# Two-layer hybrid trunk on one core: the duration estimate of a TensorE product has 32 columns added, and four planned moments are moved

## The chip, the core and the metric

The kernel runs on one core of a Trainium2 chip. The time is the device time of one execution in microseconds (us); "before" is the median of three runs. The core has TensorE (PE) for matrix products and transposes, VectorE (DVE), ScalarE (ACT) and GpSimd (POOL) for everything elementwise, and SyncE (SP), which here issues most of the DMA transfers. Each engine works through its own instruction list strictly in order; engines wait for each other by semaphores.

## The reference, cut to what matters

The input is one sequence of 512 tokens with 1024 features, float32, and two layers of parameters. Each layer computes

```
h = rmsnorm(x, norm_g);  p = h @ w_in                    # 1024 -> 3488 columns, split into 15 pieces
A: q = rmsnorm(cq) @ w_uq;  k, v = rmsnorm(ckv) @ w_ukv   # 4 heads, rope, causal softmax attention
B: o_b = c_b * short_conv(c_c * c_h, conv_w)              # width 3
C: o_c = u * (tril(sg_w) @ layernorm(v) + sg_b)           # in chunks of 128 tokens
D: q, k, v = mq, mk, mv                                   # 4 heads, rope, block-sparse attention (MoBA)
y = concat(o_a*silu(g_a), o_b*silu(g_b), o_c*silu(g_c), o_d*silu(g_d))
x = x + y @ w_out
```

Query blocks have 128 rows. With blocks of 256 keys and 512 tokens, group D's choice of blocks comes out as causal attention too.

## The kernel before, in words

**Products.** Every factor is split into a high part and a low part in the fp32r type, and each product is three PE instructions: high by high, high by low, low by high (`mm3`, L282). PE thus has 2,423 products and transposes in its list, most of them over 512 columns (tokens), the low-rank products of group A over 416, spatial mixing and some others over 256, transposes over 128.

**Weights.** They come in units of about 512 KB. SP issues the load of a unit (`load_units`, L405; the DMA itself is at L295) into one of a few raw buffers, two for most units. ACT, or DVE, makes the high part (`whi_*`), DVE the low part (`wlo_*`), into one of six pairs of split buffers (`split_units`, L442). A raw buffer is free for the next load when its split is done. An instruction that waits for a load holds up everything behind it on its engine.

**Seven-product stages.** Three groups of large products, the output projection of both layers (products `oz`, `ox`, `oy`, `ot`; weights `b`, `t`) and the token products of layer 1 (weights `p`), use a scheme with seven half-size products instead of eight. It needs sums of weight blocks, which are made in DRAM by `t_sums` (L356): SP copies a block (L367) and POOL issues accumulating DMAs onto the copy (L372). This chain starts at the moment TS0 (L2051). The products of layer 0's output projection start at place 1055 in PE's list.

**The order of the work.** The program writes out all instruction lists at build time with a planner, the class `Order` (L74). Everything is a coroutine ("chain"). The planner has one clock, `now`, which is PE's: each PE instruction adds its estimated duration. `cost(n)` gives it for a product over n columns; transposes have 109 ns written beside them. ACT, DVE, POOL and DMA have clocks with estimates of their own (`act`, `dve`, `pool`, L166 on); these are not touched. A chain that has a PE instruction to issue does this:

```
def pe(self, cost, f, *a, **k):
    if self.t != self.pe_t:
        while self.t + PEMARGIN > self.o.now:
            yield self.t + PEMARGIN
...
    self.o.now += cost
```

`self.t` is the moment at which its operands are ready by plan, so the instruction is placed at the first moment at least 80 ns (PEMARGIN) later. Until then other chains place theirs: among those that are due, `run` (L108) takes the one with the lowest priority number. The main stream has 10: the projections in the fixed orders SEQ and SEQ1 (L48, L380) and the output products. The attention heads of A (scores `sa`, softmax `pa`, its transposes `pTa` with the copies `pha` and `pla`, output `oa`) and D (the same with `d`) and other small chains have 0, so they go first as soon as they are due, and the main stream fills the gaps. How many filler products stand between two steps of an attention head thus follows from the vector engines' estimates divided by the products' estimates. ACT's and DVE's lists follow from the same clock: an instruction is emitted when the chain comes within 300 ns (SLACK) of it.

Some chains have a moment in `now` at which they may start: the mixing of group C in layer 0 (MIXT, L1904), a row of parameters (ROWT, L781 and L2049), columns of parameters (COLT, L623 and L2041) and the weight sums (TS0, L2051). Places in a list below count PE instructions from the start of the kernel.

**Names used further on.** `raw_cc`, `whi_cc`: the weights of the piece c_c, loaded and split; likewise `ch`, `gc`, `gd`, `gb`, `su`, `kv`. `zz` is the product c_c * c_h of group B on DVE, which reads the PSUM bank of `cc`. `hT` is the transposed normalised input of a layer, `a` a copy of it, and `hTh`, `hTl` its two parts. `rs_mq`, `rs_mk` are the norms of D's queries and keys, with a power on POOL. `yad`, `yD`, `ys` and `suml` are outputs of the heads and their sums ahead of the output products.

Of the kernel before, what the change touches and what calls it, by code (L numbers as in the profile page):

```python
# [32 lines left out]
WSLACK = 0.0  # L33
AHEAD, URGENT, VSLACK = 4, 2, 300.0
NWARM, FILL, FILLEND = 6, 0.9, 15000.0
MIXT, MIXLAG, ROWT, COLT = 42000.0, 2000.0, 36000.0, 17500.0
KSPLIT, HMEAN = 6, 0.0
PAIRS = {}
LOPRIO = -5
# [8 lines left out]
SEQ1 = ['p11', 'ga0', 'p21', 'p3', 'ga1', 'p4', 'p2', 'ch0', 'p1', 'p22', 'cc0', 'gd0', 'gd1', 'su0', 'gc0', 'cb0', 'gb0', 'ch1', 'cc1', 'cb1', 'gb1', 'su1', 'gc1']  # L48
K0, K1, KK = (2, 3, 0, 1), (4, 5, 6, 7), (0, 2, 3, 1)
ZPROD = ("b11", "t3", "b21", "t4", "t2", "t1", "b22")  # L50
TS0 = 62000.0
TAIL = ((0, 256), (256, 512))

C_CQ, C_KV, C_GA, C_CH, C_CB, C_CC, C_GB = 0, 256, 416, 672, 928, 1184, 1440
# [111 lines left out]
class Chain:  # L166
# [6 lines left out]
    def _emit(self, e, cost, f, a, k):  # L173
        while max(self.t, self.o.clk[e] if self.lazy else 0.0) > self.o.now + self.slack:
            yield max(self.t, self.o.clk[e] if self.lazy else 0.0) - self.slack
        self.o.clk[e] = max(self.o.clk[e], self.t, self.o.now) + cost
        self.t = self.o.clk[e] + LAT
        f(*a, **k)  # L178
# [19 lines left out]
# [4 lines that stand above are left out]
        if self.o.now < self.o.fill_until:  # L202
            for _ in range(int((self.o.now - self.o.pe_end) * FILL / (430.0 if self.o.now < 9000.0 else 220.0))):
                self.o.fill()
        self.o.now += cost
        self.o.pe_end = self.o.now
        self.t = self.pe_t = self.o.now + PELAT
        f(*a, **k)  # L208
# [5 lines left out]


def cost(n):
    return max(n / 2.4, 107.0) + 2.0


@with_exitstack  # L220
def hybrid_trunk(ctx: ExitStack, tc: tile.TileContext, x, positions, norm_g, w_c, w_f, w_t, w_o, mla_q_norm_g,
# [60 lines left out]
    def mm3(ch, n, dst, sh, sl, mh, ml, first, last, go_on=False, low=None):  # L282

        c = cost(n)
        k = dict(skip_group_check=True) if go_on else {}
        yield from ch.pe(c, PE.matmul, dst, sh, mh, start=first, stop=False, **k)
        yield from ch.pe(c, PE.matmul, dst, sh, ml, start=False, stop=False, **k)
        if low is not None:
            yield from ch.wait(low)
        yield from ch.pe(c, PE.matmul, dst, sl, mh, start=False, stop=last, **k)  # L290
# [65 lines left out]
    def t_sums(*streams):  # L356

        gap = 4000.0 if len(streams) == 1 else 3000.0
        for i in range(3):
            steps = []  # L360
            for l, src, t, b in streams:
                for n, x, y in (((f"{t}1", f"{b}11", f"{b}12"), (f"{t}3", f"{b}12", f"{b}22")),
                                ((f"{t}2", f"{t}1", f"{b}22"),), ((f"{t}4", f"{t}2", f"{b}21"),))[i]:
                    steps += [(l, src, n, x, y, j) for j in range(2)]
            for l, src, n, x, _, j in steps:
                o.clk["D"] = max(o.clk["D"], o.now) + 1500.0
                nc.sync.dma_start(src(l, n, j), src(l, x, j))  # L367
                yield o.now + gap
            yield o.now + gap
            for l, src, n, _, y, j in steps:  # L370
                o.clk["G"] = max(o.clk["G"], o.now) + 1000.0
                nc.gpsimd.dma_start(src(l, n, j), src(l, y, j), accum_op=ALU.add, max_dma_last_dim=1024)  # L372
                o.set(tsum_ev[l, n, j], o.now + 10000.0)
                yield o.now + gap
            yield o.now + (8000.0 if len(streams) == 1 else 0.0)
# [1633 lines left out]
    def start():  # L2009
        o.clk["D"] = 1000.0  # L2010
        cw = Chain(o)
        for kp in range(KT // 2):
            xk[kp] = yield from v4S.get(cw, f"x{kp}_0", [P, NT, 2 * P], F32)
        load_xk(0, 1)
        wp = yield from sS.get(cw, "warm")
        ones = one_box[0][:, 0:P].bitcast(F32)
        V.memset(ones, 1.0)
        A.activation(xsum[:, 0, 0:1], ones[:, 0:1], AF.Square, scale=D ** -0.5)
        o.fill = lambda: PE.matmul(wp[:, 0:P], ones, ones, start=True, stop=True)
        for _ in range(NWARM):  # L2020
            o.fill()
        PE.transpose(wp[:, 256:256 + NT + KT], junk[0:NT + KT, P:2 * P], ident[0:NT + KT, 0:NT + KT])
        V.tensor_copy(pg, wp[:, 256:256 + NT + KT])
        o.pe_end, o.fill_until = 3700.0, FILLEND
        o.clk["V"] = 3700.0

        def fill_end():
            o.fill_until = 0.0
            sS.put(Chain(o))
            return  # L2030
            yield
        o.spawn(fill_end(), FILLEND, -9)
        LOAD_HOOKS["c0_0"] = (lambda: load_xk(2, 4),)
        LOAD_HOOKS["c1_0"] = (lambda: load_xk(4, 6),)
        LOAD_HOOKS["c2_0"] = (lambda: load_xk(6, 8),)
        prow.append((yield from t2S.get(cw, "prow")))
        G.memset(prow[0][0:14, 0:P], 1.0)
        LOAD_HOOKS["sq0_0"] = (load_rows,)
        LOAD_HOOKS["sq1_0"] = (lambda: load_params(L0, 0),)
        LOAD_HOOKS["sq3_0"] = (lambda: load_params(L0, 1),)  # L2040
        o.spawn(param_cols(), COLT, 2)  # L2041
        for u in order[:10]:
            u.wanted = True
        o.spawn(load_units(), None, 4)
        o.spawn(split_units(0, 4), None, LOPRIO)
        o.spawn(split_units(4, len(order)), None, 5)
        o.spawn(rope_tables(), 3700.0, 4)
        o.spawn(x_stats(), None, 5)
        o.spawn(x_row(), ROWT, 5)  # L2049
        o.spawn(main(), None, 10)  # L2050
    o.spawn(t_sums((0, z_src, "t", "b"), *((l, p_src, "p", "p") for l in STOK)), TS0, 4)  # L2051
    o.spawn(start())
# [51 lines left out]
```

## Time and profile before

| | |
|---|---|
| median of 3 runs | 489.70 us (489.56 to 489.83) |
| the profiled execution's own time | 489.73 us |
| its span, first to last instruction | 488.0 us |
| TensorE's granted clock | 0.999 |
| DMA traffic | 92.89 MB, mean 190 GB/s |

A row of the waits view has the engine and group that waited, the group that released it, and then the total, the number and the longest of the waits in us. A row of a timeline has the start and the duration in us, then the engine, line and operation, output <- inputs, shapes, and in brackets the idle time before it with what ended it; consecutive equal instructions are one row with a count. Instructions of one engine overlap by their pipelines, so the cost of one in a steady stream is the distance from start to start. In the view by groups, "x | a, b" is the count, the busy time in us and the mean in ns. In the view by windows, a row has the window and its length, the busy times (with counts) of PE, its weight loads, DVE, ACT and POOL, and last the granted clock, the DMA engines' busy share and GB/s. In the view of DMA issues, the last two numbers are the size and the median time from issue to landing in us. In the chain of work that ended last, a row is the start, the length, and what ran.

### The profile page before, as it was taken

The numbers are of one execution on the slowest core, as the hardware profiler recorded it, in microseconds if no ns is written. First come the engines' busy times: TensorE is split into PE (matmuls) and PEld (weight loads), VectorE is DVE, ScalarE is ACT, GpSimd is POOL, SyncE is SP. The second block draws the span as 40 slices with busy tenths as digits, with TensorE's granted clock in tenths as the row PEclk, the third lists the DMA queues.
The fourth block names the chain that finished last, engine by engine and source line by source line (L and its number), as shares of the span: only waits on it lengthen the run. The fifth ranks groups of instructions, "written<-read, shape, count | busy, mean of one in ns | idle before, by whom it ended". The sixth has DMA issues, their size and how long they took to land.

```text
span 488.0 us, 7509 instructions
## 1 busy us (share of the span) xinstructions
PE 481.6 (99%) x2432; PEld 408.9 (84%) x2432; DVE 400.9 (82%) x893; ACT 329.9 (68%) x898; POOL 104.4 (21%) x172
## 2 busy tenths in 40 slices
PE   9999999999999999999999999999999999999997
PEld 7988888888887888888889988888888888888786
DVE  3698487668987899789998688979788998997993
ACT  5896837677546766457667788769675687666650
POOL 7855330710051210000031013620402200000000
PEclk9999999999999999999999999999999999999999
DMA  8742335897499888596574186786832744427762
GB/s 263 249 135 78 124 128 218 225 197 162 151 330 240 208 217 218 188 343 224 199 239 145 65 290 250 165 246 177 209 131 85 153 136 146 173 66 258 253 242 89
DMA packets 41904, 92.89 MB, mean 190 GB/s; under 512 B 7158, under 2 KB 23048, under 8 KB 41480
## 3 DMA queue, kind: packets, MB, share of 16 engines
q1 hardware_dynamic: 29168, 79.82, 47.3%
q0 software_dynamic: 12672, 12.58, 16.7%
q8 instruction: 19, 0.31, 0.2%
q14 instruction: 21, 0.17, 0.1%
q10 hardware_dynamic: 24, 0.01, 0.0%
HBM read 84.53 MB, written 33.03 MB: 241 GB/s over the span
## 4 chain that ended last, share of the span: by engine, by line
PE 91%; DVE 3%; ACT 2%; DMA 2%; SPq 1%; issue 1%; ACTq 0%
PE oy L208 6%; PE cq L208 6%; PE kv L208 6%; PE gb L208 5%; PE su L208 5%; PE cc L208 5%; PE sq L208 5%; PE gc L208 5%; PE ch L208 5%; PE ga L208 4%; PE oz L208 4%; PE cb L208 4%; PE py L208 3%; PE ox L208 3%; PE sa L208 3%; PE gd L208 3%
## 5 line engine op out<-in xcount | busy, mean ns | idle before, releaser
L178 ACT ACTIVATE pa<-pa,mna 128x128 f32<-128x128 f32 (+3 forms) x53 | 27.8, 554 | 5.6 <-DVE mna L178 5.5
L178 ACT ACTIVATE pd<-pd,mnd 128x384 f32<-128x384 f32 (+3 forms) x49 | 25.8, 548 | 3.2 <-DVE mnd L178 2.9
L178 ACT ACTIVATE pha<-pTa 128x512 fp32r<-128x512 f32 (+3 forms) x32 | 13.9, 434 | 20.6 <-PE pTa L208 20.4
L178 ACT ACTIVATE phd<-pTd 128x512 fp32r<-128x512 f32 (+3 forms) x32 | 13.8, 434 | 16.1 <-PE pTd L208 15.9
L178 DVE CUSTOM_DVE_ANT_0 pa<-sa,maskb,rs_q 128x512 f32<-128x512 f32 (+3 forms) x32 | 16.6, 544 | 6.2 <-PE sa L208 3.2
L178 DVE TENSOR_TENSOR wlo_p<-raw_p,whi_p 128x512 fp32r<-128x512 f32 x28 | 19.1, 698 | 2.7 <-ACT whi_p L178 2.6
L178 ACT ACTIVATE whi_t<-raw_t 128x512 fp32r<-128x512 f32 x31 | 18.2, 619 | 4.5 <-DMA raw_t<-t 4.5
L208 PE MATMUL cq<-whi_c,hTh 128*128 128x416 f32 x64 | 20.8, 370 | 0.0
L178 DVE TENSOR_TENSOR wlo_t<-raw_t,whi_t 128x512 fp32r<-128x512 f32 x32 | 20.7, 679 | 0.0
L208 PE MATMUL cq<-wlo_c,hTh 128*128 128x416 f32 x64 | 20.0, 359 | 0.0
L178 DVE TENSOR_TENSOR pla<-pTa,pha 128x512 fp32r<-128x512 f32 (+3 forms) x32 | 15.4, 485 | 5.6 <-ACT pha L178 5.6
L208 PE MATMUL cq<-whi_c,hTl 128*128 128x416 f32 x64 | 19.8, 355 | 0.0
L178 POOL TENSOR_TENSOR rs_mk<-rs_mk,nhalf 128x16 f32<-128x16 f32 x2 | 6.5, 3243 | 56.3 <-DVE rs_mk L178 56.3
L178 DVE CUSTOM_DVE_ANT_0 pd<-sd,maskb,rs_mq 128x512 f32<-128x512 f32 (+3 forms) x32 | 17.0, 545 | 1.6 <-PE pTd L208 1.0
L178 DVE TENSOR_TENSOR pld<-pTd,phd 128x512 fp32r<-128x512 f32 (+3 forms) x32 | 15.1, 485 | 3.1 <-ACT phd L178 3.0
L178 POOL TENSOR_SCALAR xss<-xss 128x1 f32<-128x1 f32 x4 | 2.7, 668 | 69.6 <-ACT jk L178 65.3
L372 POOL DMA_DIRECT2D t<-in_w_o_dram x16 | 17.0, 1341 | 2.4 <-DMA t<-t 2.3
L178 DVE TENSOR_TENSOR wlo_b<-raw_b,whi_b 128x512 fp32r<-128x512 f32 x24 | 16.0, 682 | 0.1
L178 ACT ACTIVATE whi_b<-raw_b 128x512 fp32r<-128x512 f32 x23 | 13.9, 622 | 3.1 <-DMA raw_b<-in_w_o_dram 3.0
L178 ACT ACTIVATE whi_p<-raw_p 128x512 fp32r<-128x512 f32 x22 | 13.2, 625 | 3.9 <-DMA raw_p<-in_w_t_dram 3.9
L208 PE MATMUL pTd<-ident,pd 128*128 128x128 f32 x80 | 14.1, 272 | 0.6 <-ACT pd L178 0.6
L208 PE MATMUL pTa<-ident,pa 128*128 128x128 f32 x80 | 14.0, 273 | 0.0
(473 smaller groups left out, 1846.8 us busy)
## 6 DMA issues: line engine op xcount, KB each, us to landing
t<-in_w_o_dram POOLq DMA_DIRECT2D x16, 512.0 KB, 8.3
raw_t<-t SPq DMA_DIRECT2D x16, 512.0 KB, 4.0
raw_b<-in_w_o_dram SPq DMA_DIRECT2D x12, 512.0 KB, 4.0
t<-in_w_o_dram SPq DMA_DIRECT2D x8, 512.0 KB, 4.9
p<-in_w_t_dram POOLq DMA_DIRECT2D x8, 512.0 KB, 14.0
t<-t SPq DMA_DIRECT2D x8, 512.0 KB, 4.7
raw_p<-p SPq DMA_DIRECT2D x8, 512.0 KB, 3.2
ys<-ysc SPq DMA_DIRECT2D x14, 256.0 KB, 5.0
```

What stands on the lines that cost most here:

```text
L178: f(*a, **k)
L208: f(*a, **k)
L372: nc.gpsimd.dma_start(src(l, n, j), src(l, y, j), accum_op=ALU.add, max_dma_last_dim=1024)
```

## The change

`cost(n)` becomes (n+32)/2.4 ns, at least 108, instead of n/2.4, at least 107, plus 2. For 512 columns that is 226.7 instead of 215.3, for 416 186.7 instead of 175.3, for 384 173.3 instead of 162, for 256 120 instead of 109, for 128 108 instead of 109. The four moments given in the planner's clock are raised as well (MIXT and TS0 by 4.8%, ROWT by 4.7%, COLT by 2.9%). Transposes keep 109, and the estimates of the other engines, the margins and the end of the warm-up filling (FILLEND, 15000) stay as they are.

```diff
-MIXT, MIXLAG, ROWT, COLT = 42000.0, 2000.0, 36000.0, 17500.0
+MIXT, MIXLAG, ROWT, COLT = 44000.0, 2000.0, 37700.0, 18000.0
...
-TS0 = 62000.0
+TS0 = 65000.0
...
 def cost(n):
-    return max(n / 2.4, 107.0) + 2.0
+    return max((n + 32) / 2.4, 108.0)
```

The products, the main stream's order, the transfers and what is computed stay the same. What changes is how the side chains' instructions are interleaved with the main stream on each engine, and for a few splits and squares which of ACT and DVE does them (ACT's list has 3 instructions less, DVE's one more).

## The prediction

> **What bounds the kernel now.** I read the page's first part, then the cores, the waits of TensorE (PE), and the chain that ended last.
>
> ```profile
> core 0: 488.0 us, clock 0.999
> PE 481.6 (99%) x2432; PEld 408.9 (84%) x2432; DVE 400.9 (82%) x893; ACT 329.9 (68%) x898; POOL 104.4 (21%) x172
> ```
>
> ```profile
> PE warm L2019 <- DVE ones L2017: 1.1, 1, 1.1
> PE pTd L208 <- ACT pd L178: 0.6, 1, 0.6
> PE sq L208 <- ACT krt L178: 0.6, 1, 0.6
> PE gd L208 <- DVE zz L178: 0.3, 1, 0.3
> PE oz L208 <- DVE wlo_b L178: 0.3, 1, 0.3
> ```
>
> PE is busy for 481.6 of 488.0 us at full clock. Its work is fixed, and only order can change the time: these five waits are nearly all that order costs now. The chain gives the true price of a product (start, duration, group):
>
> ```profile
> 16.28 2.26 PE cq L208 x12
> ```
>
> ```profile
> 61.03 10.88 PE ga L208 x48
> ```
>
> ```profile
> 481.72 2.88 PE ot L208 x24
> ```
>
> 10.88/48 is 226.7 ns for 512 columns, 2.26/12 is 188 for 416, 2.88/24 is 120 for 256. The old estimate says 215.3, 175.3 and 109; the new one 226.7, 186.7 and 120. So the planner's clock ran about 5% slow and is now right. Transposes keep 109, near enough: two sets of four follow each other after 0.44 us, 0.11 each.
>
> ```profile
> 73.83 0.60 PE L208 MATMUL t0a<-ident,Q 128*96 128x128 f32 x4
> 74.27 0.60 PE L208 MATMUL t1a<-ident,K 128*96 128x128 f32 x4
> ```
>
> **The change, part by part.** Nothing is added or removed on PE: both builds issue the same 2,423 products and transposes, and the same DMAs. I compared the two built instruction lists engine by engine, and turned distances in PE's list into time with the prices above.
>
> The moved moments (MIXT, ROWT, COLT, TS0) grow by 3 to 5%, as the clock does; the transposes, products and copies that they release stand at about the same products as before. I cost them at 0: PE's steady stream covers them.
>
> The longer estimate makes a product of a side chain come due after fewer products of the main stream, since the vector work between is priced as before. The attention chains get thinner in filler and finish earlier. In layer 0 the last MLA attention product goes from place 681 to 636, MoBA's from 1023 to 954 (the next stage starts at 1055). In layer 1 MLA's goes from 2003 to 1944; MoBA starts later there and ends at 2245 instead of 2260. The start of the kernel, with the first and third of the five waits, is unchanged. The other three are at places that the new order alters.
>
> *Place 1, 157 us.*
>
> ```profile
> 157.17 0.27 PE L208 MATMUL pTd<-ident,pd 128*128 128x128 f32 x1
> 158.04 0.55 PE L208 MATMUL pTd<-ident,pd 128*128 128x128 f32 x3 [0.60 <-ACT pd L178]
> ```
>
> ```profile
> 155.02 0.63 ACT L178 ACTIVATE whi_cc<-raw_cc 128x512 fp32r<-128x512 f32 x1 [2.69 <-DMA raw_cc<-in_w_f_dram]
> ```
>
> ```profile
> 148.47 6.53 DMA raw_cc<-in_w_f_dram
> ```
>
> ```profile
> raw_cc<-in_w_f_dram SPq DMA_DIRECT2D x4, 512.0 KB, 3.4
> ```
>
> The second transpose should start 0.11 after the first, at 157.28; it starts at 158.04, so 0.76 is lost. ACT, in order, stood 2.69 us before a weight split whose load took 6.53 us instead of the usual 3.4, with the attention copies queued behind it. In the built lists 17 products (3.6 us) of PE stand between that load's issue and its split before, and 33 (6.0 us) after. The 2.4 us more bring ACT's wait from 2.69 down to about 0.3; here the queue took up 2.69-0.76 = 1.93 before PE stood, so I take -0.76. If the load is longer by those 1.6 us, up to 0.76 stays.
>
> *Place 2, 343 us.* A product into gd takes the bank that the convolution's zz reads out of cc:
>
> ```profile
> 342.92 0.60 PE L208 MATMUL pTa<-ident,pa 128*128 128x128 f32 x4
> 343.86 0.50 PE L208 MATMUL gd<-hTh,whi_gd 128*128 128x512 f32 x1 [0.35 <-DVE zz L178]
> 344.20 0.40 PE L208 MATMUL gd<-hTl,whi_gd 128*128 128x512 f32 x1
> ```
>
> ```profile
> 343.12 0.69 DVE L178 SCALAR_TENSOR_TENSOR zz<-cc,chs 128x512 f32<-128x512 f32 x1 [0.25 <-PE cc L208]
> ```
>
> The four transposes end their turn at 342.92+0.44 = 343.36; gd starts at 343.86 (0.50 late) and its first product takes 0.34 instead of 0.227: 0.61. After, 21 products (3.26 us) stand between the last cc and this gd instead of the four transposes, and zz's 0.69 us lies beside them: -0.61.
>
> *Place 3, 458 us.*
>
> ```profile
> 457.62 0.61 PE L208 MATMUL oz<-whi_b,yD 128*128 128x512 f32 x2
> 458.50 0.50 PE L208 MATMUL oz<-wlo_b,yD 128*128 128x512 f32 x1 [0.26 <-DVE wlo_b L178]
> 458.83 0.40 PE L208 MATMUL oz<-whi_b,yD 128*128 128x512 f32 x1
> ```
>
> ```profile
> 450.48 0.68 DVE L178 TENSOR_TENSOR yad<-od,obd 64x512 f32<-64x512 f32 x1 [0.21 <-ACT obd L178]
> ```
>
> ```profile
> 456.82 0.41 DVE L178 TENSOR_TENSOR ys<-ys 128x256 f32<-128x256 f32 x1
> 457.16 0.68 DVE L178 TENSOR_TENSOR suml<-ys,sumh 128x512 fp32r<-128x512 f32 x1
> 457.76 0.68 DVE L178 TENSOR_TENSOR wlo_b<-raw_b,whi_b 128x512 fp32r<-128x512 f32 x1
> ```
>
> Due at 457.62+2x0.227 = 458.07, the product starts at 458.50 and takes 0.33: 0.43+0.10 = 0.53. VectorE (DVE) works back to back from the last attention output, 0.60 us from start to start per 512 columns and 0.34 per 256. After, 18 such instructions (13x0.60+5x0.34 = 9.5 us) stand between the last attention product and this one, but 52 products (11.8 us) instead of 37 (8.4 us): covered, -0.53.
>
> Removed: 0.76+0.61+0.53 = **1.90**.
>
> *New waits.* The cover of three other places gets short. (a) Layer 1's first hT transposes, near 245 us: ScalarE (ACT) has six instructions in the same 3.26 us of products instead of four. Prices, start to start:
>
> ```profile
> 250.83 0.55 ACT L178 ACTIVATE whi_c<-raw_c 128x416 fp32r<-128x416 f32 x1
> 251.26 0.60 ACT L178 ACTIVATE a<-hT 128x512 f32<-128x512 f32 x1
> 251.74 0.61 ACT L178 ACTIVATE oy<-xr 128x512 f32<-128x512 f32 x1
> ...
> 252.35 0.60 ACT L178 ACTIVATE hTh<-hT 128x512 fp32r<-128x512 f32 x1
> ```
>
> whi_c 0.43, a 0.48, oy 0.61, and hTh as a (both 0.60 long): two hTh (the first begun before the stretch, some 0.2 of it inside), two whi_c, oy and a's full 0.60 come to about 3.2 to 3.3 us. (b) The second attention product of layer 1's MLA head 2 and (c) of layer 0's MoBA head 1 stand closer behind their splits. Each is between 0 and 0.3 us, the length of the two DVE waits above; it cannot be a gain, since none of the three waits now. I take the middle: 3x0.15 = **+0.45**. A late load is a rarer kind of wait; it is between 0 and place 1's 0.76 at each place, taken as 0 here, and its other end is the second rival.
>
> DVE's load is the other worry, as denser attention asks more of it per product:
>
> ```profile
> 65.00:195.00 130.00, 129.40 (x677) 109.53 (x676) 106.76 (x249) 84.58 (x211) 25.93 (x25) 1.00 0.84 215
> ```
>
> 106.76 of 130 us is 82%; 5% more is 86%, so queues lengthen in places only.
>
> Sum against the profiled run, whose 489.73 are the span's 488.0 and 1.73 around it that the change doesn't touch: 489.73-1.90+0.45 = 488.28, and since that run lies 0.03 above the median of 489.70, **488.3** us.
>
> **A rule of the Trainium skill that speaks against the change.** "TensorE: Matmul & The Clock Gate", section "Back-to-back issue gap", gives an isolated warm gap of N/2.4+2.5 ns (216 for N=512), and less, some 131, for a sustained stream. By that the old estimate is right or too long, and the change makes every loop 5% too dense. The trace's 226.7 ns disagrees, and the measurement decides.
>
> **The rivals.**
>
> *As many waits as before.* The three gaps are accidents of one order, and another order has its own. Slack shrinks by 5% in all attention loops, so beyond (a) to (c) some three more waits of 0.3 to 0.6 us arise: 488.3+1.4 = 489.7. For it: every loop is touched. Against: PE stops only three times for order now, and I found three short covers, not six.
>
> *Slower, by late loads.* The POOL queue runs an attention step and behind it the accumulating copies for the later seven-product stages:
>
> ```profile
> 88.64 2.91 POOL L178 TENSOR_TENSOR rs_mq<-rs_mq,nhalf 128x16 f32<-128x16 f32 x1 [22.57 <-DVE rs_mq L178]
> 91.50 4.41 POOL L372 DMA_DIRECT2D t<-in_w_o_dram  x4
> 94.30 5.75 POOL L372 DMA_DIRECT2D p<-in_w_t_dram  x4
> ```
>
> ```profile
> t<-in_w_o_dram POOLq DMA_DIRECT2D x16, 512.0 KB, 8.3
> ```
>
> ```profile
> p<-in_w_t_dram POOLq DMA_DIRECT2D x8, 512.0 KB, 14.0
> ```
>
> In the new order that step comes some 8 us of products earlier, so these copies run beside the loads of gc0 and ch0. gc0's split on ACT stands only 3.6 us of products behind its load: if loads take 6.5 us again, ACT blocks as at place 1, for up to 0.76 of PE each time. It decides from three such blocks on (2.3 us against the 1.45 gained; 490.6), and with four it gives 491.3. I put it at 491.0. For it: the DMA engines are 84% busy in this stretch (next to last column). Against: in the old order this one load alone stopped PE.
>
> *The change does not do what it says:* by the page's rule the clock would now run 5% fast, loops would be too dense, and a wait of 0.3 us, the length of place 3's, would appear in about half of the 16 heads: 488.3+2.4 = 490.7. Against it stand the three products' prices above.
>
> **How the numbers follow.** A measurement of this kernel tells about 0.2% (0.98 us) from no change: faster means under 488.72, slower over 490.68. Forecast 488.3: 0.48. As many waits: 0.31. Late loads: 0.20; a too dense clock: 0.01. So faster 0.48, same 0.31, slower 0.21. All three gaps gone with no new wait is 487.8, and one more small gap might go: low end 487.4. The high end takes in three to four late loads: 491.2. The forecast's own range is 487.8 to 488.7.
>
> **What would show it.** In the new profile's PE waits, the rows pTd on pd, gd on zz and oz on wlo_b are gone; warm and sq stay. If (a) to (c) are right, hT waits on an ACT copy near 245 us and oa or od on pla or pld, 0.1 to 0.3 us each. Layer 0's last od should end some 15 us sooner. The first rival shows as many short PE waits on DVE or ACT, the second as ACT whi waits on raw loads between 70 and 100 us with PE waits behind them. I would be wrong if PE's idle time grows, or if one wait, at a bank or a queue that I did not count, exceeds 1 us.

## The result: slower, and the profile after

The changed kernel takes 491.30 us (median of 14 runs, 490.34 to 494.34) against 489.71 of before (488.88 to 492.06): ratio 1.0038, 95% interval 1.0020 to 1.0055. The prediction said 488.3. The profiled execution took 490.93, with a span of 489.2 us. The runs of the changed kernel spread more than those of before, and the two longest (494.34 and 493.95) have a mean granted clock of 0.995 and 0.996; the last section comes back to that. One run of e7 below, 683.43 us at a granted clock of 0.656, is left out of its ratio.

The waits of TensorE in the changed kernel (engine, group, what released it; total, number, longest):

```profile
PE warm L2019 <- DVE ones L2017: 1.1, 1, 1.1
PE pTd L208 <- DVE pd L178: 1.1, 2, 0.6
PE sq L208 <- ACT krt L178: 0.7, 1, 0.7
PE cq L208 <- ACT hTh L178: 0.3, 1, 0.3
PE oy L208 <- DVE xr L178: 0.2, 1, 0.2
PE xT L208 <- DMA x<-in_x_dram: 0.2, 1, 0.2
```

The three waits that were forecast to go (pTd on ACT, gd, oz) are gone. Four others stand in their place. Where the time came from is best seen by three stretches, between fixed places in the trace's list of PE records (counted from 0, with the warm-up products, so these places are nine higher than the prediction's). Place 228 lies near 46 us, where the start of the kernel ends; 1220, near 247 us, is the first hT transpose of layer 1; 2431 is the last. Ahead of each of them both kernels have done the same products and transposes, in another order:

| start of | before | changed | difference of the stretch |
|---|---|---|---|
| place 228 | 46.33 | 46.53 | +0.20 |
| place 1220 | 246.34 | 247.50 | +0.96 |
| place 2431 | 484.31 | 485.50 | +0.03 |

**Layer 0.** Two transposes of one attention step come late, and what made them late is a load, just as at 157 us before. PE's timeline, then ACT's, then the chain of work:

```profile
146.59 0.39 PE L208 MATMUL gd<-hTh,wlo_gd 128*128 128x512 f32 x1
147.51 0.30 PE L208 MATMUL pTd<-ident,pd 128*128 128x128 f32 x1 [0.54 <-DVE pd L178]
148.36 0.60 PE L208 MATMUL pTd<-ident,pd 128*128 128x128 f32 x3 [0.55 <-DVE pd L178]
```

```profile
144.72 0.63 ACT L178 ACTIVATE whi_gb<-raw_gb 128x512 fp32r<-128x512 f32 x1 [2.73 <-DMA raw_gb<-in_w_f_dram]
```

```profile
136.19 8.50 DMA raw_gb<-in_w_f_dram
144.72 0.63 ACT whi_gb L178
145.35 1.49 ACT pd L178 x6
146.86 0.19 DVE mnd L178
147.08 0.29 DVE pd L178
147.36 0.66 DVE chs L178
148.02 0.29 DVE pd L178
148.36 0.60 PE pTd L208 x3
```

The first pTd is due at 146.59+0.227 = 146.82 and starts 0.69 late; the next is due 0.11 later and starts 0.74 late: 1.43 us. A load of gb that took 8.50 us held ACT for 2.73 us; the softmax steps of pd stood behind it on ACT, and the transposes wait for DVE's steps behind those. The load of cc, which cost 0.76 us at 157 us before and was to be relieved, indeed costs nothing any more. These two make +0.67; the other 0.3 of the stretch lies in steps of about 0.1 us and less.

**Layer 1.** gd and oz (1.14 us) are gone. In their place stand two hT transposes near 256 us (0.25 together), two score products and one product of oy:

```profile
394.33 0.39 PE L208 MATMUL gb<-hTh,wlo_gb 128*128 128x512 f32 x1
394.75 0.50 PE L208 MATMUL sd<-mk0d,mq0d 128*128 128x512 f32 x1
```

```profile
393.36 0.63 ACT L178 ACTIVATE whi_cb<-raw_cb 128x512 fp32r<-128x512 f32 x1
394.01 0.68 ACT L178 ACTIVATE mk0d<-tmkd,pcol 64x512 fp32r<-64x512 f32 x1
```

```profile
473.86 0.39 PE L208 MATMUL oy<-whi_t,suml 128*128 128x512 f32 x1
474.46 0.47 PE L208 MATMUL oy<-whi_t,sumh 128*128 128x512 f32 x1 [0.22 <-DVE xr L178]
```

The score product sd stands 0.19 late and its first product takes 0.11 more, since mk0d ran on ACT behind a weight split (the same again at 400 us: 0.29); oy starts 0.38 late. That is about 1.2 us for 1.14.

### The profile page after: what moved, and what is told of

Its sections match the earlier page's. It is cut to its first block, busy times and chain, and to the rows that moved or that the text cites. A ratio compares the mean times of both kernels' runs of the same rounds, so it can differ in the third digit from the quotient of the medians.

```text
span 489.2 us, 7512 instructions
## 1 busy us (share of the span) xinstructions
PE 482.0 (99%) x2432; PEld 407.5 (83%) x2432; DVE 401.8 (82%) x894; ACT 330.1 (67%) x891; POOL 106.0 (22%) x172
## 4 chain that ended last, share of the span: by engine, by line
PE 86%; DVE 7%; DMA 3%; ACT 2%; issue 1%; SPq 0%
PE cq L208 6%; PE kv L208 6%; PE oy L208 5%; PE sq L208 5%; PE su L208 5%; PE gb L208 5%; PE cb L208 5%; PE ga L208 4%; PE gc L208 4%; PE gd L208 4%; PE ch L208 3%; PE cc L208 3%; PE py L208 3%; PE sa L208 3%; PE oz L208 2%; PE pz L208 2%
## 5 line engine op out<-in xcount | busy, mean ns | idle before, releaser
L178 ACT ACTIVATE pd<-pd,mnd 128x512 f32<-128x512 f32 (+3 forms) x51 | 27.1, 556 | 2.7 <-DVE mnd L178 2.2
L178 ACT ACTIVATE pa<-pa,mna 128x128 f32<-128x128 f32 (+3 forms) x45 | 23.9, 553 | 3.8 <-DVE mna L178 3.5
L178 ACT ACTIVATE whi_p<-raw_p 128x512 fp32r<-128x512 f32 x25 | 14.9, 623 | 2.4 <-DMA raw_p<-in_w_t_dram 2.4
L208 PEld LDWEIGHTS pTd<-ident,pd 128*128 128x128 f32 x80 | 10.3, 140 | 4.8 <-issue 0.9
```

## The experiments

Time stretches in the table are worked out as above, each from one trace of its kernel; "0-228" is the start of place 228. The same work stands ahead of place 1220 in all twenty traces. Ahead of place 228, e2, e13 and e17 have one or two other products of 512 columns, and e14 another order. The expectations count the second stretch to place 1300, so it is given too, but not all kernels have done the same there: the changed kernel and e1, e3, e6, e8, e10 to e15, e17 and e18 have four transposes ahead of place 1300 where the others have four products of 416 columns. That makes their figure 0.4 us too small against the others'.

| kernel | 0-228 | 228-1220 | 1220-2431 | 228-1300 | span | median, ratio to before (95%) |
|---|---|---|---|---|---|---|
| before | 46.33 | 200.01 | 237.97 | 213.74 | 488.0 | 489.71 |
| changed | 46.53 | 200.97 | 237.99 | 214.82 | 489.2 | 491.30, 1.0038 (1.0020-1.0055) |
| e1 | 47.04 | 199.84 | 238.03 | 213.69 | 488.6 | 490.54, 1.0019 (1.0006-1.0031) |
| e2 | 45.81 | 200.58 | 238.05 | 214.30 | 488.2 | 489.75, 1.0004 (0.9993-1.0015) |
| e3 | 47.23 | 199.38 | 238.01 | 213.24 | 488.3 | 489.74, 0.9998 (0.9987-1.0010) |
| e4 | 46.17 | 199.23 | 238.03 | 212.95 | 487.1 | 489.29, 0.9993 (0.9983-1.0003) |
| e5 | 47.03 | 201.56 | 238.24 | 215.31 | 490.5 | 492.45, 1.0059 (1.0044-1.0073) |
| e6 | 46.05 | 205.15 | 239.49 | 218.97 | 494.4 | 495.97, 1.0136 (1.0107-1.0165) |
| e7 | 46.26 | 200.25 | 238.14 | 213.96 | 488.4 | 489.68, 0.9995 (0.9984-1.0006) |
| e8 | 45.67 | 206.20 | 238.01 | 220.06 | 493.6 | 494.05, 1.0089 (1.0067-1.0110) |
| e9 | 46.14 | 200.12 | 238.65 | 213.85 | 488.6 | 491.61, 1.0034 (1.0019-1.0049) |
| e10 | 47.49 | 200.47 | 237.97 | 214.32 | 489.6 | 491.03, 1.0029 (1.0017-1.0040) |
| e11 | 45.88 | 206.11 | 237.99 | 219.97 | 493.7 | 494.57, 1.0099 (1.0081-1.0117) |
| e12 | 46.53 | 199.00 | 237.99 | 212.85 | 487.2 | 488.83, 0.9984 (0.9975-0.9993) |
| e13 | 45.57 | 199.79 | 238.04 | 213.61 | 487.1 | 488.82 (one run) |
| e14 | 46.12 | 201.28 | 238.04 | 215.13 | 489.2 | 490.87 (one run) |
| e15 | 46.55 | 204.07 | 238.01 | 217.92 | 492.3 | 494.01, 1.0071 (1.0052-1.0089) |
| e16 | 46.22 | 200.10 | 237.99 | 213.82 | 488.0 | 490.38, 1.0006 (0.9995-1.0016) |
| e17 | 45.90 | 199.90 | 237.97 | 213.73 | 487.5 | 489.24, 0.9989 (0.9980-0.9998) |
| e18 (changed again) | 46.99 | 203.24 | 238.01 | 217.10 | 492.0 | 491.98, 1.0045 (1.0028-1.0062) |

The theories: **A**, a weight load beside the accumulating DMAs of the weight sums is late, holds ACT or DVE, and so PE; **B**, thinner attention loops by themselves; **C**, the moved moments. From e5 on, **S** stands for a loss in the start by the new order of ACT and DVE there.

### e1, e2: the estimate alone, the moments alone

e1 is the changed kernel with `MIXT, MIXLAG, ROWT, COLT = 42000.0, 2000.0, 36000.0, 17500.0` and `TS0 = 62000.0`; e2 is the kernel before with the four new values.

> The new estimate with the four old moments. Theory A (a late load): what costs time in the changed kernel is a weight load that runs beside the accumulating DMAs of the second weight sum; here those sums start at 62 instead of 65 us of the planner's clock, some three products of the main stream earlier against the loads, so the 1.44 us lost at 147 us (load of gb 8.5 us long, ScalarE held 2.7 us by it, two transposes of pd late) should change its place or size: 489.5 to 491. Theory B (thin loops: the longer estimate leaves 5% less filler in every attention loop, moments don't matter): the same time as the changed kernel, 491.3, with the pTd wait of 1.4 us in place. Theory C (the moved moments cost it): 489.7.

> The old estimate with the four new moments. Theory A: the sums start later against the old order, so the 0.76 us lost at 157 us moves to another load: between 489.0 and 490.5, with the gd (0.6) and oz (0.5) gaps of before unchanged. Theory B: as before, 489.7. Theory C: 491.3.

The lists of PE, ACT and DVE of e1 are those of the changed kernel, instruction by instruction (buffer numbers apart); only SP's and GpSimd's transfers come in another order. With that alone, ACT's wait for gb falls from 2.7 to 1.6 us and the loss at 147 us from 1.43 to 0.29:

```profile
ACT whi_gb L178 <- DMA raw_gb<-in_w_f_dram: 1.6, 1, 1.6
```

So that loss does not follow from the order of the engines alone (against B); the transfers that run beside the load decide it. What the estimate alone costs in e1's trace lies in the start (0.71 us); its layer 0 is as fast as that of before (199.84 against 200.01). The moments alone cost nothing (against C): e2 is where before is, with the pTd gap moved from 157 to 189 us (0.85). The ratios of e1 and the changed kernel have overlapping intervals, and one trace each says little about a load whose length changes from run to run (e18 below): the weight of the argument is on e3 and e12.

### e3, e4: the second sums' additions left out

```diff
-                nc.gpsimd.dma_start(src(l, n, j), src(l, y, j), accum_op=ALU.add, max_dma_last_dim=1024)
+                if i != 1:
+                    nc.gpsimd.dma_start(src(l, n, j), src(l, y, j), accum_op=ALU.add, max_dma_last_dim=1024)
```

> The changed kernel with the four accumulating DMAs of the second sums (t2, p2) left out; the copies stay, so the sums lack a term. Theory A: the load of gb falls from 8.5 us to 3.5 to 4.5, ScalarE's wait of 2.7 us and the two pTd waits go: 1.44 us less than the changed kernel, a span of about 487.8 instead of 489.2. Theory B: the pTd waits stay, 489.2.

> The kernel before with the same four accumulating DMAs left out. Theory A: the load of cc falls from 6.5 us to about 3.5, and the 0.76 us at 157 us go: a span of 487.2 instead of 488.0. Theory B: the pTd wait stays, 488.0.

The edit leaves out six of the 24 accumulating DMAs, four between 132 and 148 us and two in layer 1. As theory A said: in e3 the pTd waits and ACT's wait for gb are gone and places 228 to 1220 take 1.59 us less than in the changed kernel; in e4 the gap at 157 us is gone and they take 0.78 less than before, though by the medians e4 gains only 0.44 us, with an interval that takes in no gain. e3's median is 489.74 where the changed kernel has 491.30, though its start was 0.7 us slower in its trace. And without these additions the new order takes nearly as long in layer 0 as the old one (199.38 and 199.23): for theory B's thinner loops that leaves 0.15 us. The DMA rows of the kernel before for the 16 us around its late load (queue: packets, MB, share of the 16 engines) show how heavy these transfers are:

```profile
q0 software_dynamic: 2025, 2.02, 78.9%
q1 hardware_dynamic: 422, 1.81, 30.8%
```

The software queue carries the accumulating transfers (in e12, which has none, it moves nothing), the hardware queue the loads. Packet by packet the former are small (2.02 MB in 2,025), and the time of their packets adds up to 79% of all DMA engines' time, for about the bytes that the hardware queue moves with 31%.

### e5 to e8: the new estimate in parts of the kernel

```diff
-        self.o.now += cost
+        self.o.now += cost - (32 / 2.4 - 2.0) * (cost > 109.5 and not LO <= self.o.npe < HI); self.o.npe += 1
```

LO and HI are 0 and 205 in e5, 205 and 1290 in e6, 1290 and the end in e7, 205 and the end in e8; `npe` counts the planner's PE instructions.

> The new estimate for the first 205 PE instructions (some 41 us), the old one behind; moments 44000, 37700, 18000 and 64000 (shifted by what the clock gains up to there). Theory S (the new lists of ScalarE and VectorE cost 0.2 to 1.0 us in the start, since the second half of a weight unit's split now stands ahead of hTh and waits for the load): PE's place 228 comes at 46.4 to 47.2 us as in the three traces of the new lists, not at 45.8 to 46.3 as in the three of the old ones. The rest is an order of its own: 489.5 to 491. Rival (the start differs by chance between executions): place 228 at 45.8 to 46.3.

> The new estimate from PE instruction 205 to 1290 (the rest of layer 0), the old one before and behind; old moments but TS0 at 63000. Theory S: place 228 at 45.8 to 46.3 us. Theory A (late loads beside the second sums): a pTd wait of 0.3 to 1.4 us near 147 us, behind a load of gb or cc of over 6 us. Layer 1 as before: gd 0.6 and oz 0.5. In all 489.5 to 490.8. Theory B (thin loops) gives PE waits on DVE or ACT steps of attention in layer 0 that no load explains.

> The new estimate from PE instruction 1290 on; old moments. All lists are those of before up to there, so the start and the 0.76 us at 157 us are those of before. Theory B' (in layer 1 the change trades the gd and oz gaps, 1.14 us, for waits of hT, sd and oy, 1.23 us in the changed kernel's trace): 489.7, same as before. The prediction's count (three short covers of 0.15) would give 489.0.

> The new estimate from PE instruction 205 on; moments 42000, 36000, 17500 and 63000. Theory S: place 228 at 45.8 to 46.3 us and 0.7 us less than the new estimate everywhere with the same luck of the loads: 489.9 to 490.6. Rival (chance): 490.5 to 491.3.

*Start.* e5 reached place 228 at 47.03, e6 to e8 at 45.67 to 46.26, as theory S said. Six traces have the changed kernel's PE list up to there and ten the list of before. The new lists give 46.53 to 47.49 (mean 47.05), the old ones 45.67 to 46.55 (mean 46.18): **0.87 us**, of which the first profile happened to show only 0.20. The two PE lists are the same up to place 172, and behind it they take the same time up to 228 (12.49 us before and changed), so the loss lies ahead of that, where ACT's list differs from 10 us on.

e5's whole time, 492.45, is a miss all the same: behind the start its order loses 1.33 us at 159 us, behind a load of cc that took 5.97 us beside the additions, and 0.68 at 83 us.

*Layer 1.* e7, whose lists are those of before up to layer 1, is where before is (0.9984 to 1.0006): an even trade.

*Layer 0.* e6 and e8 came out 4 to 6 us slower than I expected, in the main by one event near 92 us. In e8, GpSimd's step for rs_mq came early and let the additions go, and a load of gc met them. GpSimd, the chain, DVE and PE:

```profile
76.87 2.92 POOL L178 TENSOR_TENSOR rs_mq<-rs_mq,nhalf 128x16 f32<-128x16 f32 x1 [11.77 <-DVE rs_mq L178]
79.74 3.38 POOL L372 DMA_DIRECT2D t<-in_w_o_dram  x3
```

```profile
82.90 8.85 DMA raw_gc<-in_w_f_dram
```

```profile
91.77 0.43 DVE L178 CAST whi_gc<-raw_gc 128x512 fp32r<-128x512 f32 x1 [5.27 <-DMA raw_gc<-in_w_f_dram]
```

```profile
93.00 0.47 PE L208 MATMUL sa<-hi1a,hi0a 96*128 96x512 f32 x1 [1.79 <-DVE hi1a L178]
94.83 0.79 PE L208 MATMUL sa<-lo1a,hi0a 96*128 96x512 f32 x1 [1.36 <-DVE lo1a L178]
```

That is the prediction's second rival, at its own place, though in a kernel made for something else. e6 also shows two waits of 0.8 us in layer 1. The one at 401 us is an event of the same kind: the chain of work leads back to a load of cb that took 8.56 us (from 390.26 us) beside two accumulating DMAs of layer 1's sums, issued at 388 us. At 352 us no load stands in the chain; there DVE has a weight split (wlo_su, 0.60 us) ahead of the attention step that PE waits for.

### e9 to e12, e15, e16: the sums moved, or left out

e9 is before with `TS0 = 30000.0`, e10 the changed kernel with it, e11 e8 with it; e12 is e8 with all accumulating DMAs left out (`if i > 2:` ahead of them). e15 is e8 with `TS0 = 76000.0`, e16 before with `TS0 = 73000.0`. In e9, e11, e15 and e16 the lists of PE, ACT and DVE don't change by this.

> The kernel before with TS0 at 30000 instead of 62000: the lists of PE, ScalarE and VectorE are those of before to the instruction, only the order of SP's and GpSimd's transfers changes; the sums start some 30 us sooner and the accumulating DMAs meet other loads. Theory A (what a given order loses in layer 0 is set by which weight load runs beside the accumulating DMAs): the 0.76 us at 157 us go, other loads may be hit instead: PE's places 228 to 1300 take 213.0 to 214.5 us (before 213.7; 213.0 without the second sums' additions), 489.0 to 490.5 in all. Theory B (thin loops): nothing changes, 213.7 and 489.7.

> The changed kernel with TS0 at 30000 instead of 65000; PE's, ScalarE's and VectorE's lists are nearly those of the changed kernel. Theory A: the 1.44 us at 147 us go and places 228 to 1300 take about 213.3 us instead of 214.8 unless another load is hit; the start (place 228 at 46.4 to 47.2 us) stays slow: about 490.0. Theory B: 214.8 and 491.3.

> The new estimate from PE instruction 205 on with TS0 at 30000 instead of 63000; PE's, ScalarE's and VectorE's lists are those of that kernel at 63000. Theory A: the load of gc that took 8.85 us and held VectorE for 5.3 us at 92 us meets no addition, so the 5 to 6 us lost between 90 and 101 us go: 488.5 to 489.5, the fastest of the versions. Theory B (the order of the vector engines itself is bad): 493 to 494 as at 63000.

> The new estimate from PE instruction 205 on, TS0 at 63000, with all accumulating DMAs left out; the copies stay, so all the sums lack their second term. Theory A: the load of gc at 83 us falls from 8.85 us to 3.5 to 4.5, no PE wait over 0.4 us is left in layer 0 behind place 228: places 228 to 1300 in 213.0 to 213.4 us, 488.3 to 489.0 in all. Theory B: 493 to 494.

> The new estimate from PE instruction 205 on with TS0 at 76000 instead of 63000; PE's, ScalarE's and VectorE's lists are those at 63000, the sums start some 13 us later, behind the load of gc. Theory A: that load takes 3.5 to 5 us instead of 8.85 and the 5 us at 92 us go: places 228 to 1300 in 213 to 214.5 us, 488.8 to 490.3 in all, by whether another load is hit. Theory B: 493 to 494.

> The kernel before with TS0 at 73000 instead of 62000; PE's, ScalarE's and VectorE's lists unchanged. Theory A: the 0.76 us at 157 us are traded for another place or go: places 228 to 1300 in 213.0 to 214.5 us, 489.0 to 490.5. Theory B: 213.7 and 489.7.

e12 is the clearest: the very lists of PE, ACT and DVE that took 494.05 us in e8 take 488.83 without the additions, less than before, with gc's load at 3.6 us. e11 was a miss: earlier sums did not dodge. GpSimd works in order, rs_mq stood in the middle of the sums and waited until 77 us for its input, and the rest went out behind it, beside gc again (9.20 us):

```profile
65.27 3.38 POOL L372 DMA_DIRECT2D t<-in_w_o_dram  x3
77.09 2.94 POOL L178 TENSOR_TENSOR rs_mq<-rs_mq,nhalf 128x16 f32<-128x16 f32 x1 [8.45 <-DVE rs_mq L178]
80.00 1.05 POOL L372 DMA_DIRECT2D t<-in_w_o_dram  x1
80.68 4.50 POOL L372 DMA_DIRECT2D p<-in_w_t_dram  x4
```

e15's time is a miss too. Nothing is lost at 92 us any more, but a load of gb beside the later sums takes 6.09 us and costs 0.89 at 147 us, and three waits of 0.7 to 1.4 us for splits of b and t between 222 and 232 us take back most of what was won. That the late sums cause these three is likely, but not shown. In e10 the loss at 147 us is 0.73 instead of 1.43, where theory A expected none, and its time is a us over the expected one. e9 and e16 change the gap at 157 us from 0.76 to 0.41; e9 loses 0.5 at 78 us and some 0.7 in layer 1, e16 0.3 at 228 us. e9's timed runs fall in two groups (489.87 to 490.33, 491.61 to 492.02) and its trace is from the lower one; what the upper one lost is open.

### e13, e14, e17: the start

The edit of e5 with `cost > 109.5 and self.o.npe < 100` for e13 and e17, and `cost > 109.5 and 100 <= self.o.npe < 205` for e14, in the changed kernel.

> The old estimate for the first 100 PE instructions, the new one behind; moments of the changed kernel. Only the start is read: if the split half that stands ahead of hTh is what costs (up to place 132), place 132 comes at 25.3 to 25.95 us as in the old lists and place 228 at most some 0.5 us later than theirs, 46.0 to 46.5. If the cost lies behind place 100, place 228 comes at 46.4 to 47.2.

> The new estimate for the first 100 PE instructions, the old one up to 205, the new one behind; moments of the changed kernel. If the split half ahead of hTh costs, place 132 comes at 25.9 to 26.3 us as in the new lists, and place 228 at 46.4 or later. If the cost lies behind place 100: place 228 at 45.7 to 46.3.

> The old estimate for the first 100 PE instructions, the new one behind, timed. If the first look holds (start 0.6 us shorter than in the old lists' mean, places 228 to 1300 in 213.6 us, no load beside the additions that holds PE over 0.3 us): 488.6 to 489.2, ratio 0.998 to 0.999. If it was luck of the loads: 489.5 to 490.5.

Place 132 comes at 25.59 (e13) and 25.95 us (e17) with the old estimate in the first 100 products, at 26.27 (e14) with the new one. Old lists gave 25.35 to 26.15 there (mean 25.8), new ones 25.9 to 26.9 (mean 26.3): the ranges overlap, the means speak for the first 100. e13's place 228 (45.57) came sooner than expected. e14's (46.12) missed its expectation: its PE list no longer has sq late by 0.9 us on krt. What happens in the first 100 is seen on ACT, before and changed:

```profile
13.25 0.55 ACT L178 ACTIVATE whi_c<-raw_c 128x416 fp32r<-128x416 f32 x1 [0.35 <-DMA raw_c<-in_w_c_dram]
...
14.11 0.67 ACT L178 ACTIVATE hTh<-xT,pg 128x512 fp32r<-128x512 f32 x1
14.68 0.54 ACT L178 ACTIVATE whi_c<-raw_c 128x416 fp32r<-128x416 f32 x1
```

```profile
12.60 0.55 ACT L178 ACTIVATE whi_c<-raw_c 128x416 fp32r<-128x416 f32 x1 [0.15 <-DMA raw_c<-in_w_c_dram]
...
13.46 0.54 ACT L178 ACTIVATE whi_c<-raw_c 128x416 fp32r<-128x416 f32 x1
...
14.30 0.67 ACT L178 ACTIVATE hTh<-xT,pg 128x512 fp32r<-128x512 f32 x1
```

With a longer estimate the second half of a unit's split is due before hTh. It now stands ahead of it, and hTh, which PE's next products need, is as late as the load. In e3's trace PE waits for it three times:

```profile
PE cq L208 <- ACT hTh L178: 1.2, 3, 0.5
```

The same view of before shows no such row. But only the third of these waits, at 12.45 us, stands where the order of ACT differs, and a late load makes such a wait in the old order as well (e15: 0.8 us in two waits, e17: 1.1 in two). The means tell more. At places 53 and 69, where hTh now stands behind the second half, PE comes 0.61 us late in the six new lists and 0.08 in the ten old ones; in e14 it is 0.65, in e13 and e17 0.15 and nothing. Smaller pieces of the 0.87 us lie behind the first 100: 0.17 at place 152 and 0.13 at 161, where sq comes 0.90 late in every new list and 0.76 in every old one; at place 130 the new lists win 0.16. Another 0.21 lies at place 37, ahead of which ACT's order is the same in both, so it isn't of the order; the loads may be it.

e17 is the **version that beats both**, if by little: 489.24 us, ratio 0.9989 (0.9980 to 0.9998) to before. Its longest wait in layer 0 behind place 228 is 0.31 us.

### e18: the changed kernel again

> The changed kernel once more. Place 228 at 46.4 to 47.5 us; a pTd wait of 0.3 to 1.5 us near 147 us behind the load of gb, whose length changes from execution to execution; layer 1 (from place 1300 on) 224.1 to 224.2 us with the same waits of hT, sd and oy. In all 490.5 to 491.5.

Start and layer 1 came as expected; layer 0 lost more (203.24 against 200.97). The same load of gb took 9.23 us and held ACT for 3.47 us, and pTd's first transposes were 1.40 and 0.79 late.

## Why the prediction was wrong, step by step

- **Bound and prices: right.** The same PE work in the same steady stream; only waits moved.
- **Places 2 and 3 (-0.61, -0.53): right**, both gone.
- **Place 1 (-0.76): the step that failed.** The gap did go, but the sentence "A late load is a rarer kind of wait ... taken as 0 here" was wrong: what made that load late, the additions of the second sums beside it, was still there and met the next load in the new order. Here 1.43 us came, 2.2 and more in e18. I had counted how many products cover one load instead of asking what had made it last 6.53 us. e3, e4 and e12 show the cause.
- **"The start of the kernel ... is unchanged": failed.** I had compared PE's list only, which is the same up to place 172; ACT's and DVE's lists there are not. 0.87 us on average, 0.53 of it where hTh stands behind the second half of a split.
- **New waits (+0.45): mis-sized.** (a) came, 0.25 for two sets of hT; (b) 0.1; (c) not at all. The two sd waits (0.59) and oy (0.38) I did not see. Layer 1 as a whole is an even trade (+0.03 in the profile; e7).
- **Sum.** Forecast -1.45; the profile shows +0.20+0.96+0.03 = +1.19. With the start's mean of 0.87 instead of 0.20 it would be 1.86; the medians differ by 1.59.
- **Rivals.** "Late loads" had the mechanism; its place (70 to 100 us) was that of e8 and e11, while the changed kernel is hit at 136 to 145. Its price, up to 0.76 us for each load, was too low: one load cost 1.43 here and, with the clock's fall shown below, some 6 in e8. "As many waits" describes layer 1.

## What to carry to other kernels

A more truthful estimate in a planner doesn't make a better order if what decides is outside its model: here its DMA clock knows bytes, not that accumulating transfers slow the loads beside them. When a wait goes because its place moves, ask what made the awaited thing late, and where that will strike next. Compare the lists of all engines, not only the bound one's: an instruction that stands ahead of another and waits for a load makes both late.

## What the runs showed of the hardware that I had not expected

**A short halt of PE can cost as much again by the clock.** In e18 the two waits at 147 us are followed by half speed. PE's timeline, then windows (start:end, length, busy times of PE, its loads, DVE, ACT, GpSimd; granted clock; DMA share, GB/s):

```profile
148.68 0.30 PE L208 MATMUL pTd<-ident,pd 128*128 128x128 f32 x1 [1.23 <-DVE pd L178]
149.57 0.82 PE L208 MATMUL pTd<-ident,pd 128*128 128x128 f32 x3 [0.60 <-DVE pd L178]
150.04 0.78 PE L208 MATMUL gd<-hTh,whi_gd 128*128 128x512 f32 x1
150.61 0.63 PE L208 MATMUL gd<-hTl,whi_gd 128*128 128x512 f32 x1
151.04 0.63 PE L208 MATMUL gd<-hTh,wlo_gd 128*128 128x512 f32 x1
```

```profile
147.00:149.50 2.50, 0.74 (x3) 0.15 (x2) 1.44 (x5) 2.50 (x9) 1.53 (x2) 1.00 1.12 288
149.50:152.80 3.30, 3.23 (x11) 2.74 (x12) 2.93 (x7) 1.19 (x4) 0.00 (x0) 0.53 1.24 196
```

The granted clock falls to 0.53 for 3.3 us, and a product of 512 columns takes 0.43 us (150.61 to 151.04) instead of 0.227; the delays behind 149.6 us add up to 1.5 us. Waits of 0.54 and 0.55 at the same place in the first profile cost no clock, nor did single ones of 1.15 to 1.24 us in e5, e14 and e15 (granted clock 1.00 behind each). The Trainium skill ("TensorE: Matmul & The Clock Gate", section "What's actually happening") puts the fall to half clock after at least one idle window of about 3.4 us; here PE was busy 0.74 of 2.5 us, with no single halt over 1.23 us, and it fell. In e8 the waits of 1.79 and 1.36 us are followed by a stretch at 0.50:

```profile
96.00:101.40 5.40, 5.40 (x20) 4.82 (x19) 3.10 (x8) 1.57 (x4) 1.01 (x1) 0.50 1.24 204
```

All six runs of e8 have a granted clock of 0.993 to 0.997, so it is no accident of one run there.

A fall of the clock fits the two longest of the changed kernel's 14 runs, whose clocks of 0.995 and 0.996 are those of e18's profile (0.996), but they have no trace, so it isn't shown for them.
